# RWKV-7 recurrence of a hybrid decoder layer: each head on its own 64 rows, with block-diagonal operands

## The chip, the cores and the metric

The kernel runs on one core of a Trainium2 chip. The time is the device time in microseconds (us) of one execution. It is given as the median of several runs. A profile is one further execution, recorded by the hardware profiler; its times come from that execution alone. The engines in it are PE (the matrix engine; PEld is its weight loading), DVE (vector), ACT (scalar), POOL (GpSimd) and SP, which here only starts transfers.

## The reference, cut to what matters

One decoder layer for 1024 new tokens (and 8 single-token sequences that are handled apart): RMSNorm, one input projection, three parallel head groups (RWKV-7, HGRN2, RG-LRU), one output projection, then a squared-ReLU MLP with 4096 hidden columns, and a last norm. The change touches the RWKV-7 group: 6 heads of 64 channels, with a 64 by 64 state per head.

```python
k = k * (1.0 + (a - 1.0) * k_a)
def step(S, inp):
    rt, wt, kt, vt, kkt, at = inp
    sa = jnp.einsum('bhvk,bhk->bhv', S, -kkt)
    S = S * wt[:, :, None, :] + sa[..., None] * (kkt * at)[:, :, None, :] + vt[..., None] * kt[:, :, None, :]
    return S, jnp.einsum('bhvk,bhk->bhv', S, rt)
S_T, out = lax.scan(step, S0, (tm(r_h), tm(w_h), tm(k_h), tm(v_h), tm(kk), tm(a_h)))
gn = ((out - mean) * lax.rsqrt(var + GN_EPS)).reshape(B, T, c) * ln_w + ln_b
bonus = (jnp.sum(r_h * k_h * r_k, -1, keepdims=True) * v_h).reshape(B, T, c)
return (gn + bonus) * g, S_T
```

## The kernel before

The layer runs in two stretches. In the **first**, `weave` (L83) mixes seven streams of work with a filler, which is the dense work of the projections: input projections `in`, output projections `out`, and the first two MLP tiles. The order of PE's instructions is the order in which `weave` issues them. It keeps a modelled PE clock `now`, which `mm` (L71) and `tr` (L76) advance, and every `yield D` in a stream says by how much of that clock the stream should come back later; until then other streams or dense products are issued. The instructions of DVE, ACT and POOL are put in order by the compiler's scheduler, and each engine then runs its own list strictly in that order. In the **second** stretch, the MLP (`up`, `dn`) and the last norm run with nothing to weave.

The dense products are float32 split into a high and a low half (`xh`, `xl`, `wh`, `wl`), three products of one pass each. All small products of the recurrence are plain float32; one such product shows up as two matmul records in the trace, called halves below.

The recurrence is worked in 12 parts: 3 pairs of heads times 2 halves of the sequence times 2 quarters of 256 tokens. A part has 4 chunks of 64 tokens (`C` = 64, `NQ` = 4). The channels of the two heads of a pair lie on rows 0 to 63 and 64 to 127. Four streams share a part:

- `rw_operands` (L491) makes the operands. It needs the inverse root of the sums of squares of k: a product `pc_kk`, the value `ir_kk` on DVE (L245), its power on POOL (L129), a copy `t` on DVE (L248), and two transposes on PE into `pb_kk`, which DVE reads at L517. The decay and rate parts are the products `pw` and `pa`, with 64 rows each of `waup`. Then `kb` holds the two scaled key-like operands for one chunk; `kbt` is their transpose (4 transposes, copied by ACT at L560), and `uv` gets the transpose of v.
- `rw_inverse` (L574) computes the masked 64 by 64 tables: `sc` (L591) from `kb` and `ar` with 8 products, each 64 rows by 128 columns; then 6 levels that multiply a 64 by 64 inverse together (`W`, copied by ACT at L621; `Y`, merged by DVE at L636). Last it makes `mv`, 8 products with v.
- `rw_chain` (L652) goes through the chunks in order, as each needs the state `st` of the one before. Each step has three places on PE with a DVE operation behind each: `ch` from `st` and `ar`, then DVE's `rh` (L670); `ch` from `rh` and `ym`, then DVE's copy into `uv` (L676); then three groups together: `uv` with `kbt` (the new state, DVE's `st` at L697, with POOL's `ws` at L691), `st` with `ar`, and `uv` with `sc` (the outputs). The 128 rows carry alternate chunks here: `brow` and `krow` say which 64 rows a chunk sits on. The state is a 128 by 128 tile with zeros off the diagonal.
- `rw_finish` (L713) normalises the outputs, transposes them (`oT`), and writes them into `mix`.

A PE instruction uses the array in a tile size (rows by columns, in the profile "128\*128", "64\*64" and so on). The dense products and the transposes use 128\*128. The small ones before use 64\*64, 128\*64, 64\*128 or 32\*32.

Weights are staged by `load_w` (L255): a raw float32 tile by DMA, a copy and a difference into the high and low half. The raw tile has two buffers.

Of the kernel before, what the change touches and what calls it, by code (L numbers as in the profile page):

```python
# [51 lines left out]
def kernel(ctx: ExitStack, tc: tile.TileContext, i, o):  # L52
# [172 lines left out]
    waup = const.tile([P, 384], F32, name="waup")  # L225
# [29 lines left out]
    def load_w(src, name, kt=KT, wpool=wpool, dst=None, parts=1):  # L255


        raw = wpool.tile([P, kt, P], F32, tag=f"raw{kt}", name=f"raw_{name}", bufs=2)
        wh, wl = dst or (wpool.tile([P, kt, P], F32R, tag=f"{q}{kt}", name=f"{q}_{name}", bufs=2) for q in ("wh", "wl"))
        for g in range(parts):  # L260
            ks = slice(g * kt // parts, (g + 1) * kt // parts)
            nc.sync.dma_start(raw[:, ks], src[:, ks])
            act(wh[:, ks], raw[:, ks], AF.Copy)  # L263
            if name in SOON:
                V.tensor_tensor(wl[:, ks], raw[:, ks], wh[:, ks], op=ALU.subtract)  # L265
# [182 lines left out]
    lora, rkv = {}, {}  # L448
    sm = {nm: hgp.tile([P, 3, NB], F32, name=f"sm_{nm}") for nm in "rkv"}
# [23 lines left out]
    rw_st = [[rwp.tile([P, P], F32, name=f"st{j}_{q}") for q in range(2)] for j in range(3)]  # L473
    for st in rw_st:
        for q in range(2):
            G.memset(st[q], 0.0)
    brow = (slice(64, 128), slice(0, 64))
    krow = (slice(0, 64), slice(64, 128))
# [6 lines left out]
    def units():  # L485

        for h in range(2):
            for c in range(NQ):
                yield c, h, brow[c % 2], slice(((c // 2) * 2 + h) * C, ((c // 2) * 2 + h) * C + C)

    def rw_operands(q):  # L491
# [20 lines left out]
        mm(pw[:, 0:QT], waup[0:64, jc], xwa[0:64, qs])  # L512
# [8 lines left out]
        mm(pa[:, 0:QT], waup[64:128, jc], xwa[64:128, qs])  # L521
# [16 lines left out]
        for c in range(NQ // 2):
            tr(pt[:, c * P:(c + 1) * P], v[:, q0 + c * P:q0 + (c + 1) * P], ident)
        pt4 = pt[:, 0:NQ // 2 * P].rearrange("p (c x) -> p c x", x=P)  # L540
        S.copy(uv[0:64, 0:NQ:2, :], pt4[0:64])
        S.copy(uv[64:128, 1:NQ:2, :], pt4[64:128])
        ck4 = "p (c x t) -> p c x t"
        V.scalar_tensor_tensor(t5, t3, 1.0, t4, op0=ALU.add, op1=ALU.mult)
        V.scalar_tensor_tensor(kb[:, :, 1:3, :], t5.rearrange(ck4, x=2, t=C), 0.5, t1.rearrange(ck4, x=2, t=C),
                               op0=ALU.mult, op1=ALU.mult)
        V.tensor_scalar(t3, t3, hka[:, j:j + 1], omka[:, j:j + 1], op0=ALU.mult, op1=ALU.add)
        V.tensor_tensor(t3, t3, k_, op=ALU.mult)
        V.tensor_tensor(kb[:, :, 0:4:3, :], t3.rearrange(ck4, x=2, t=C), t1.rearrange(ck4, x=2, t=C), op=ALU.mult)
# [10 lines left out]
        S.copy(kbt, pt.rearrange("p (c x) -> p c x", x=P))  # L560
# [5 lines left out]
        mm(pb, bones, t5)  # L566
# [3 lines left out]
        live[q] = dict(ee=ee, ar=ar, kb=kb, kbt=kbt, uv=uv, bo=bo)  # L570
# [3 lines left out]
    def rw_inverse(q):  # L574
# [4 lines left out]
        ar, kb, uv = (live[q][x] for x in ("ar", "kb", "uv"))  # L579

        sc = rwp.tile([P, 2 * NQ, P], F32, tag="sc", name=f"sc_{n}", bufs=3)
        ym, xm = (w2(nm, n, 3).rearrange("p (u t) -> p u t", t=C) for nm in ("ym", "xm"))
        (S.copy if q < 2 else G.tensor_copy)(ym, bc(id64[:, None, :], [P, NQ, C]))
        for h in range(2):
            hp = slice(h * 64, h * 64 + 64)
            pt = ps("ra", f"sc{h}_{n}")
# [17 lines left out]
        for l in range(1, 6):  # L604
# [4 lines left out]
            pt = ps("ra", f"W{l}_{n}")[:, 0:QT]  # L609
            pt3 = pt.rearrange("p (u t) -> p u t", t=C)  # L610
            for c, h, b, cc in units():
                if last:
                    u, b0 = cc.start // C, b.start
                    mm(pt3[b0 + 32:b0 + 64, u, 0:32], sc[b0:b0 + 32, 2 * c + h, 32:64], xm[b0:b0 + 32, u, 0:32])
                else:
                    mm(pt[b, cc], sc[b, 2 * c + h, 0:64], xmf[b, cc])
# [25 lines left out]

        yield D14
# [4 lines left out]
        live[q].update(sc=sc, ym=ym, xm=xm)  # L648
# [3 lines left out]
    def rw_chain(q):  # L652
# [4 lines left out]
        ee, ar, kbt, uv, sc, ym, xm = (live[q][x] for x in ("ee", "ar", "kbt", "uv", "sc", "ym", "xm"))  # L657
        pt = ps("ch", f"ch_{n}")
        po = pt[:, QT:2 * QT]
        for c in range(NQ):  # L660
            st = rw_state[j]
            b = brow[c % 2]
            first = st is None
            mv = xm[b, (c // 2) * 2:(c // 2) * 2 + 2, :].rearrange("p h v -> p (h v)")
            if first:
                rh = mv
            else:
                mm(pt[b, 0:P], ar[:, c, 0, :], st)
                rht = rwp.tile([P, P], F32, tag="rh", name=f"rh{c}_{n}", bufs=1)
                V.tensor_tensor(rht[b, :], pt[b, 0:P], mv, op=ALU.add)  # L670
                rh = rht[b, :]
# [6 lines left out]
            for h in range(2):  # L678
# [5 lines left out]
            for h in range(2):  # L684
                hp = slice(h * 64, h * 64 + 64)
                mm(out[:, hp], sc[:, 2 * c + h, 64:128], uv[:, c, hp], start=first, stop=first or h == 1)
            wc = ee[:, c, C:C + 1]
            sn = rw_st[j][c % 2]
            if not first:
                ws = rwp.tile([P, P], F32, tag="ws", name=f"ws{c}_{n}", bufs=2)  # L690
                G.tensor_scalar(ws, st, wc, 0.0, op0=ALU.mult, op1=ALU.add)  # L691
            for h in range(2):
                hp = slice(h * 64, h * 64 + 64)
                if first:
                    V.tensor_scalar(sn[hp, hp], pt[hp, P:P + 64], wc[hp], None, op0=ALU.mult)
                else:
                    V.scalar_tensor_tensor(sn[hp, hp], pt[hp, P:P + 64], wc[hp], ws[hp, hp], op0=ALU.mult, op1=ALU.add)  # L697
# [15 lines left out]
    def rw_finish(q):  # L713
# [5 lines left out]
        ot, sums, bo = (live[q][x] for x in ("ot", "sums", "bo"))  # L719
        V.tensor_scalar(sums[:, 0], sums[:, 0], -1.0 / 64.0, None, op0=ALU.mult)  # L720
        sq = small.tile([P, 64], F32, tag="gsq", name=f"gsq_{n}", bufs=1)
        for g in range(NQ):
            act(sq, ot[:, g * 64:(g + 1) * 64], AF.Square, bias=sums[:, 0, g:g + 1],
# [828 lines left out]
```

## Time and profile before

| | before |
|---|---|
| median of 3 runs | 1618.23 us (1614.12 to 1618.76) |
| the profiled execution | 1615.32 us |
| its span, first to last instruction | 1613.5 us |
| mean granted PE clock | 0.967 |
| PE busy, whole span | 95% |
| DVE, ACT, POOL busy, whole span | 48%, 39%, 23% |
| PE busy, DVE busy, ACT busy from 250 to 410 us | 154.8, 107.7, 79.0 of 160 us |
| PE busy, DVE busy, ACT busy from 890 us to the end | 714.0, 202.6, 225.1 of 723 us |

A profile line of a group reads: source line, engine, operation, what is written "<-" what is read (names without buffer numbers), the tile size on PE, the shape, the count, then busy time and the mean duration in ns, then idle time ahead of it and what ended it. A line of the timeline reads: start in us, duration in us, engine, line, operation, names, count. Durations of PE records overlap, since matmuls are pipelined: what one costs is the distance from start to start.

### The profile page before, as it was taken

What the parts mean: (1) busy time and instruction counts of PE and PEld (TensorE: products, weight loads), DVE (VectorE), ACT (ScalarE), POOL (GpSimd) and SP (SyncE); (2) the same over time, 40 slices, a digit from 0 to 9 for tenths busy, and PEclk for the clock granted to TensorE, in tenths of its full rate; (3) what the DMA queues carried; (4) which work ended last, traced back from release to release, by engine and by line L of the source; (5) the groups of instructions that cost most, each with busy time, mean ns of one, the idle gap of its engine ahead of it and who ended that gap; (6) DMA issues with size and microseconds to landing.
All of it is one profiled execution on the core that took longest, in us unless ns stands there. A gap on an engine that the chain in (4) does not pass through costs nothing. (4 is left out here: it accounts for less than half of the span.)

```text
span 1613.5 us, 29358 instructions
## 1 busy us (share of the span) xinstructions
PE 1534.4 (95%) x12158; PEld 1310.5 (81%) x12158; DVE 775.8 (48%) x1765; ACT 637.1 (39%) x1361; POOL 376.9 (23%) x492
## 2 busy tenths in 40 slices
PE   8879899999899999899987999999999999999997
PEld 6657677688788788777787889989898989899887
DVE  7476656775656676675465222222232222222224
ACT  4444633653445355355344323233232423233232
POOL 4462312322323423423222010111101010111111
PEclk8979989999799999999999999999999999999999
DMA  6524424333243434434433353545445353544342
GB/s 216 134 53 95 90 67 92 80 80 86 60 91 75 100 80 101 99 81 113 113 119 103 82 109 80 108 85 104 83 101 92 79 110 81 104 85 89 58 90 106
DMA packets 54501, 152.18 MB, mean 94 GB/s; under 512 B 7104, under 2 KB 7392, under 8 KB 54368
## 3 DMA queue, kind: packets, MB, share of 16 engines
q0 software_dynamic: 24416, 70.67, 26.3%
q1 hardware_dynamic: 29808, 79.61, 15.3%
q8 instruction: 95, 1.56, 0.4%
q14 instruction: 38, 0.31, 0.1%
q10 hardware_dynamic: 144, 0.04, 0.0%
HBM read 144.12 MB, written 6.17 MB: 93 GB/s over the span
## 5 line engine op out<-in xcount | busy, mean ns | idle before, releaser
L74 PE MATMUL in<-xh,wl_in 128*128 128x512 f32 (+3 forms) x648 | 226.3, 349 | 6.5 <-DMA wl_in<-in_w_in 6.5
L74 PE MATMUL in<-xl,wh_in 128*128 128x512 f32 (+3 forms) x648 | 224.4, 346 | 3.4 <-DVE xl L357 3.4
L74 PE MATMUL in<-xh,wh_in 128*128 128x512 f32 (+3 forms) x648 | 225.4, 348 | 0.0
L74 PE MATMUL dn<-hh,wl_w 128*128 128x264 f32 (+2 forms) x696 | 223.3, 321 | 0.2 <-DMA wl_w<-in_w 0.2
L74 PE MATMUL dn<-hh,wh_w 128*128 128x264 f32 (+2 forms) x696 | 223.0, 320 | 0.0
L74 PE MATMUL dn<-hl,wh_w 128*128 128x264 f32 (+2 forms) x696 | 223.0, 320 | 0.0
L1440 DVE TENSOR_TENSOR mix<-mix,dn 128x512 f32<-128x512 f32 (+2 forms) x192 | 98.4, 512 | 241.6 <-PE dn L74 241.6
L268 POOL DMA_DIRECT2D wl_w<-in_w x88 | 76.3, 874 | 577.3 <-ACT hh L1370 323.6
L263 ACT ACTIVATE wh_w<-raw_w 128x512 fp32r<-128x512 f32 (+1 forms) x90 | 70.6, 784 | 272.5 <-PE dn L74 224.5
L1369 DVE SCALAR_TENSOR_TENSOR rl<-up,rl 128x512 f32<-128x512 f32 (+2 forms) x96 | 49.6, 516 | 222.3 <-ACT rl L1368 222.3
L74 PE MATMUL up<-nxh,wh_w 128*128 128x264 f32 (+1 forms) x512 | 145.7, 285 | 1.5 <-DVE rl L1369 1.3
L74 PEld LDWEIGHTS in<-xh,wl_in 128*128 128x128 f32 x648 | 128.2, 198 | 22.5 <-DMA wl_in<-in_w_in 8.0
L74 PE MATMUL up<-nxl,wh_w 128*128 128x264 f32 (+1 forms) x512 | 145.0, 283 | 0.5 <-POOL nxl L1268 0.5
L74 PE MATMUL up<-nxh,wl_w 128*128 128x264 f32 (+1 forms) x512 | 145.2, 284 | 0.0
L74 PEld LDWEIGHTS dn<-hh,wl_w 128*128 128x128 f32 x696 | 131.0, 188 | 13.8 <-DMA wl_w<-in_w 3.8
L74 PEld LDWEIGHTS in<-xl,wh_in 128*128 128x128 f32 x648 | 127.8, 197 | 17.5 <-DVE xl L357 4.3
L74 PEld LDWEIGHTS in<-xh,wh_in 128*128 128x128 f32 x648 | 128.6, 198 | 15.8 <-issue 4.7
L74 PEld LDWEIGHTS dn<-hl,wh_w 128*128 128x128 f32 x696 | 131.1, 188 | 10.0
L74 PEld LDWEIGHTS dn<-hh,wh_w 128*128 128x128 f32 x696 | 131.2, 188 | 9.2
L74 PE MATMUL up<-nh,wl_w 128*128 128x512 f32 x256 | 102.7, 401 | 5.9 <-DMA wl_w<-in_w 5.9
L1368 ACT ACTIVATE rl<-up 128x512 f32<-128x512 f32 (+2 forms) x96 | 43.3, 451 | 152.4 <-PE up L74 152.4
L74 PE MATMUL up<-nh,wh_w 128*128 128x512 f32 x256 | 102.6, 401 | 0.0
(438 smaller groups left out, 3215.8 us busy)
## 6 DMA issues: line engine op xcount, KB each, us to landing
raw_in<-in_w_in SPq DMA_DIRECT2D x53, 512.0 KB, 3.4
wl_in<-in_w_in POOLq DMA_DIRECT2D x49, 512.0 KB, 5.6
raw_w<-in_w SPq DMA_DIRECT2D x32, 512.0 KB, 3.3
raw_w<-in_w SPq DMA_DIRECT2D x64, 256.0 KB, 2.7
wl_w<-in_w POOLq DMA_DIRECT2D x30, 512.0 KB, 5.4
wl_w<-in_w POOLq DMA_DIRECT2D x58, 256.0 KB, 4.1
raw_out<-in_w_out SPq DMA_DIRECT2D x16, 512.0 KB, 3.4
wl_out<-in_w_out POOLq DMA_DIRECT2D x8, 512.0 KB, 5.6
```

The lines of the kernel that those rows point to most:

```text
L74: PE.matmul(out, lhsT, rhs, start=start, stop=stop)
L263: act(wh[:, ks], raw[:, ks], AF.Copy)
L268: G.dma_start(wl[:, ks], src[:, ks], accum_op=ALU.add)
L1368: act(rl[:, :n], pt[:, :n], AF.Relu)
L1369: V.scalar_tensor_tensor(rl[:, :n], pt[:, :n], 0.0, rl[:, :n], op0=ALU.max, op1=ALU.mult)
L1440: V.tensor_tensor(x2[m][:, c0:c0 + n], x2[m][:, c0:c0 + n], pt[:, :n], op=ALU.add)
```

## The change

Each head stays on its own 64 rows throughout, and operands are put on a diagonal of two 64 by 64 blocks, with zeros beside them, so that one product of the whole 128 by 128 array serves both heads:

- `kz` (the two key operands), `az` and `yz` (copies of `ar`'s first half and of `ym`) are block diagonals. They exist once each, and their zero blocks are written once at the start. `wup` and `aup` are the two halves of `waup` with zeros in the other rows.
- In a step of the chain each of the three places is one product of 128 rows and 128 columns against 64 moving columns. The output products (`st` with `ar`, `mv` and `vr` with `sr`) leave the step and stand together at the part's end, 24 products of 64\*64.
- The products with v move: the product `mv` leaves the end of `rw_inverse` and runs beside `W` at level 1, and a new product `kt` with `vr`, scaled by the chunk's decay `wc`, beside `W` at level 2. The state update then adds that `kv` on POOL, in a second operation.
- Transposes: of v 4 for 2, of the keys 8 (`bt`, `kt`) for 4, of the output 4 for 2. ACT has new copies: v doubled into `bt`, two each for `vr`, `kt`, `yz`, `az`.
- The buffers of `raw8` and `ee` are fewer (2 to 1, 3 to 1), and six weight tiles of the last MLP block take other buffers.

The core of the diff:

```diff
-    rw_st = [[rwp.tile([P, P], F32, name=f"st{j}_{q}") for q in range(2)] for j in range(3)]
-    brow = (slice(64, 128), slice(0, 64))
-    krow = (slice(0, 64), slice(64, 128))
+    rw_st = [[rwp.tile([P, C], F32, name=f"st{j}_{q}") for q in range(2)] for j in range(3)]
+    kz = rwp.tile([P, 2, NQ, 2, C], F32, name="kz")
+    az = rwp.tile([P, NQ, 2, C], F32, name="az")
+    yz = rwp.tile([P, NQ, 2, C], F32, name="yz")
...
-        mm(pw[:, 0:QT], waup[0:64, jc], xwa[0:64, qs])
+        mm(pw[:, 0:QT], wup[:, jc], xwa[:, qs])
...
+        S.copy(bt.rearrange("p c (h t) -> p c h t", t=C), twice(v_))
+        for c in range(NQ):
+            tr(pt[:, c * P:(c + 1) * P], bt[:, c], ident)
+        heads_of(vr, pt)
...
+        for c in range(NQ):
+            tr(pt[:, c * P:(c + 1) * P], kz[:, 0, c].rearrange("p h t -> p (h t)"), ident)
+        S.copy(bt, pt.rearrange("p (c x) -> p c x", x=P))
+        yield D4
+        pt = ps("o", f"kt_{n}")
+        for c in range(NQ):
+            tr(pt[:, c * P:(c + 1) * P], kz[:, 1, c].rearrange("p h t -> p (h t)"), ident)
+        heads_of(kt, pt)
...
-                mm(pt[:, c * P:(c + 1) * P],
-                   kb[hp, c // 2, 2 * (c % 2):2 * (c % 2) + 2, :].rearrange("p x t -> p (x t)"),
-                   ar[hp, c, :, :].rearrange("p x t -> p (x t)"))
+                mm(pt[:, c * P:(c + 1) * P], kz[:, g, c].rearrange("p h t -> p (h t)"), ar[:, c].rearrange("p x t -> p (x t)"))
...
+            if l <= 2:
+                for c, h, b, cc in units():
+                    mm(px[b, cc], kv[b, c] if l == 1 else kt[b, c], vr[b, c])
...
-        pt = ps("ra", f"mv_{n}")[:, 0:QT]
-        for c, h, b, cc in units():
-            mm(pt[b, cc], sc[krow[c % 2], 2 * c + h, 0:64], uv[krow[c % 2], c, h * 64:h * 64 + 64])
-        S.copy(xmf, pt)
...
+        for h, b in enumerate(brow):
+            S.copy(yz[b, :, h], ym[b])
+            S.copy(az[b, :, h], ar[b, :, 0])
...
-                mm(pt[b, 0:P], ar[:, c, 0, :], st)
+                mm(pa, az[:, c].rearrange("p h t -> p (h t)"), st)
...
-            for h in range(2):
-                hc = slice(h * 64, h * 64 + 64)
-                mm(pt[b, hc], ym[b, (c // 2) * 2 + h, :], rh[:, hc])
-            V.tensor_copy(uv[b, c, :], pt[b, 0:P])
+            mm(pu, yz[:, c].rearrange("p h t -> p (h t)"), rh)
+            V.tensor_copy(mv[:, c], pu)
             yield D17
-            for h in range(2):
-                hp = slice(h * 64, h * 64 + 64)
-                mm(pt[hp, P:P + 64], kbt[:, c, hp], uv[:, c, hp])
-            out = po[krow[c % 2], (c // 2) * P:(c // 2) * P + P]
-            if not first:
-                mm(out, ar[:, c, 1, :], st, stop=False)
-            for h in range(2):
-                hp = slice(h * 64, h * 64 + 64)
-                mm(out[:, hp], sc[:, 2 * c + h, 64:128], uv[:, c, hp], start=first, stop=first or h == 1)
+            mm(pst, bt[:, c], mv[:, c])
...
+                G.tensor_scalar(ws, st, wc[:, c:c + 1], 0.0, op0=ALU.mult, op1=ALU.add)
+                G.tensor_tensor(ws, ws, kv[:, c], op=ALU.add)
+            V.scalar_tensor_tensor(sn, pst, wc[:, c:c + 1], ws, op0=ALU.mult, op1=ALU.add)
...
             if c == NQ - 1:
+                for c_, h, b, cc in units():
+                    terms = ([(ar[b, c_, 1], sts[c_][b])] if sts[c_] is not None else []) + [(sr[b, g, c_], x[b, c_]) for g, x in enumerate((mv, vr))]
+                    for u, (w, x) in enumerate(terms):
+                        mm(po[b, cc], w, x, start=u == 0, stop=u == len(terms) - 1)
```

What this does to the order of the instructions, at three places. First PE's list, in the second step of the first part's chain; in its rows an `in` row is a dense product, and the shape behind the names is that of the operand in rows by columns. Before:

```order
L74 MATMUL ch_0_0_1299<-rh_0_0_0_1356,ym_0_0_751 64x64 x2
L74 MATMUL in_0_0_1384<-xl_224,wh_in_0_1258 128x512
L74 MATMUL in_0_0_1384<-xh_216,wl_in_0_1259 128x512
L74 MATMUL in_0_0_1384<-xh_217,wh_in_0_1258 128x512
L74 MATMUL in_0_0_1384<-xl_225,wh_in_0_1258 128x512
L74 MATMUL gram_0_0_1403<-rq_188,kq_0_0_1330 64x2x32 x8
L74 MATMUL Y_0_0_1_1413<-ym_0_1_990,wm_0_0_1_1358 64x64 x8
L74 MATMUL ch_0_0_1299<-uv_0_0_639,kbt_0_0_638 64x64 x2
L74 MATMUL ch_0_0_1299<-st_0_176,ar_0_0_636 64x128
L74 MATMUL ch_0_0_1299<-uv_0_0_639,sc_0_0_750 64x64 x2
```

Now, the same step:

```order
L74 MATMUL ch_0_0_1356<-rh_0_0_0_1464,yz 128x64
L74 MATMUL in_0_0_1428<-xh_227,wh_in_0_1285 128x512
L74 MATMUL in_0_0_1428<-xl_235,wh_in_0_1285 128x512
L74 MATMUL in_0_0_1428<-xh_227,wl_in_0_1286 128x512
L74 MATMUL in_0_0_1428<-xh_228,wh_in_0_1285 128x512
L74 MATMUL W_0_0_1_1488<-xm_0_1_1096,sa_0_1_1094 64x64 x8
L74 MATMUL gram_0_0_1498<-rq_197,kq_0_0_1433 64x2x32 x8
L74 MATMUL pc_kk_0_0_1508<-bones,t_1_0_0_1473 128x2 x2
L74 MATMUL ch_0_0_1356<-mv_0_0_806,bt_0_0_646 128x64
```

The two products with `ym` are one with `yz`, and of the five products at the end of the step one is left; the products of the outputs have moved to the end of the part.

Second, POOL's list early on, where the power `ir_kk` for the second part stands. The `mix` rows with `xrb` are the input's normalisation for the second half of the sequence (eight multiplications, then eight scalings). Before:

```order
L891 TENSOR_SCALAR hf_0_624<-hf_0_624,nfA,fA 128x512
L346 TENSOR_TENSOR mix_69<-mix_69,xrb 128x520
L346 TENSOR_TENSOR mix_70<-mix_70,xrb 128x520
L129 TENSOR_TENSOR ir_kk_0_1_789<-ir_kk_0_1_789,mhalf 128x4
L346 TENSOR_TENSOR mix_71<-mix_71,xrb 128x520
```

Now:

```order
L349 TENSOR_TENSOR mix_76<-mix_76,xrb 128x520
L350 TENSOR_SCALAR mix_69<-mix_69,vt 128x520
L350 TENSOR_SCALAR mix_70<-mix_70,vt 128x520
L946 TENSOR_TENSOR kq_0_0_1065<-kq_0_0_1065,hf_0_632 128x256
L350 TENSOR_SCALAR mix_71<-mix_71,vt 128x520
L350 TENSOR_SCALAR mix_72<-mix_72,vt 128x520
L129 TENSOR_TENSOR ir_kk_0_1_846<-ir_kk_0_1_846,mhalf 128x4
```

The power stood behind two of the eight multiplications; it stands behind all eight, four scalings and one `kq` now.

Third, DVE's list at the copy `t` that follows this power and that PE's transposes `pb_kk` read. Rows of `lgq`, `lxb`, `lxc` and `lcar` belong to the RG-LRU stream, rows of `kq` and `rq` to HGRN2. Before:

```order
L1142 SCALAR_TENSOR_TENSOR lxc_0_666<-lgq_0_504,lxc_0_666 128x512
L591 TENSOR_TENSOR sc_0_0_750<-sc_0_0_0_796,cmask 128x4x128
L598 COPY_PREDICATED ym_0_0_751<-cmask,sc_0_0_750 64x256 x2
L248 COPY t_0_0_1_738<-ir_kk_0_1_789 128x256
L602 STREAM_TRANSPOSE xm_0_0_752<-ym_0_0_751 128x256
```

Now:

```order
L941 TENSOR_TENSOR kq_0_0_1159<-b_0_1052 128x512
L1167 TENSOR_SCALAR lgq_0_513<-lgq_0_513 128x512
L949 TENSOR_TENSOR rq_197<-kq_0_0_1159,hq_0_705 64x256 x2
L1169 SCALAR_TENSOR_TENSOR lgq_0_513<-lgq_0_513,lxc_0_679 128x512
L1171 SCALAR_TENSOR_TENSOR lxc_0_679<-lxb_0_511,lgq_0_513 128x512
L1175 SCALAR_TENSOR_TENSOR mix_75<-lgl_0_512,lxc_0_679 128x512
L1179 COPY lcar<-lxc_0_679 128x1
L251 COPY t_0_0_1_796<-ir_kk_0_1_846 128x256
```

The copy (L248, now L251) has moved behind the next level of HGRN2 (`kq_0_0_1159`, whose buffer is the one that `xrb` held, so that it follows the last of POOL's multiplications) and behind the end of the first RG-LRU piece, which includes a square root on ACT.

More of the change, by code (lines that the diff above doesn't have):

```diff
@@ L223 @@
     V.tensor_scalar(nsp2, sp2, -2.0, None, op0=ALU.mult)
-    waup = const.tile([P, 384], F32, name="waup")
+    wup, aup = (const.tile([P, 384], F32, name=nm) for nm in ("wup", "aup"))
+    G.memset(wup[64:128], 0.0)
+    G.memset(aup[0:64], 0.0)
     gup = const.tile([P, 384], F32, name="gup")
@@ L255, in load_w @@
     def load_w(src, name, kt=KT, wpool=wpool, dst=None, parts=1):
-        raw = wpool.tile([P, kt, P], F32, tag=f"raw{kt}", name=f"raw_{name}", bufs=2)
+        raw = wpool.tile([P, kt, P], F32, tag=f"raw{kt}", name=f"raw_{name}", bufs=1 if kt == KT else 2)
         wh, wl = dst or (wpool.tile([P, kt, P], F32R, tag=f"{q}{kt}", name=f"{q}_{name}", bufs=2) for q in ("wh", "wl"))
@@ L504, in ck, with heads_of @@
             return ap.rearrange("p (c t) -> p c t", t=C)
+        def heads_of(out, pt):
+            for h, b in enumerate(brow):
+                S.copy(out[b], pt[b].rearrange("p (c h x) -> p c h x", h=2, x=C)[:, :, h])
         r_, k_, v_ = r[:, qs], k[:, qs], v[:, qs]
-        t1, t2, t3, t4, t5 = (w2(f"t{u}", n, 1) for u in range(1, 6))
+        t1, t2, t3, t4 = (w2(f"t{u}", n, 1) for u in range(1, 5))
         act(t2, k_, AF.Square, scale=vec("kk", j))
         pw = ps("o", f"pw_{n}")
-        mm(pw[:, 0:QT], waup[0:64, jc], xwa[0:64, qs])
+        mm(pw[:, 0:QT], wup[:, jc], xwa[:, qs])
         act(t1, pw[:, 0:QT], AF.Tanh, bias=hw0[:, j:j + 1], scale=0.5)
@@ L535, in rw_operands @@
         act(t1, t2, AF.Exp, scale=-1.0)
+        V.tensor_copy(wc, ee[:, :, C])
         pt = ps("o", f"vT_{n}")
[L538 to L546, printed above, removed]
+        S.copy(bt.rearrange("p c (h t) -> p c h t", t=C), twice(v_))
+        for c in range(NQ):
+            tr(pt[:, c * P:(c + 1) * P], bt[:, c], ident)
+        heads_of(vr, pt)
+        V.scalar_tensor_tensor(t2, t3, 1.0, t4, op0=ALU.add, op1=ALU.mult)
+        for h, b in enumerate(brow):
+            V.scalar_tensor_tensor(kz[b, 0, :, h], ck(t2[b]), 0.5, ck(t1[b]), op0=ALU.mult, op1=ALU.mult)
         V.tensor_scalar(t3, t3, hka[:, j:j + 1], omka[:, j:j + 1], op0=ALU.mult, op1=ALU.add)
         V.tensor_tensor(t3, t3, k_, op=ALU.mult)
-        V.tensor_tensor(kb[:, :, 0:4:3, :], t3.rearrange(ck4, x=2, t=C), t1.rearrange(ck4, x=2, t=C), op=ALU.mult)
+        for h, b in enumerate(brow):
+            V.tensor_tensor(kz[b, 1, :, h], ck(t3[b]), ck(t1[b]), op=ALU.mult)
         V.scalar_tensor_tensor(ar[:, :, 0, :], ck(t4), -1.0, ee[:, :, 0:C], op0=ALU.mult, op1=ALU.mult)
@@ L569, in rw_operands @@
             free["pm"] += 3
-        live[q] = dict(ee=ee, ar=ar, kb=kb, kbt=kbt, uv=uv, bo=bo)
+        live[q] = dict(wc=wc, ar=ar, bt=bt, kt=kt, vr=vr, bo=bo)
         ev(("A2", q), L_EV)
@@ L621, in rw_inverse @@
                 S.copy(wm, pt)
+            if l <= 2:
+                px3 = px.rearrange("p (c t) -> p c t", t=C)
+                if l == 1:
+                    S.copy(mv, px3)
+                else:
+                    V.tensor_tensor(kv, px3, bc(wc[:, :, None], [P, NQ, C]), op=ALU.mult)
             yield D12
@@ L656, in rw_chain @@
         yield ("B", q)
-        ee, ar, kbt, uv, sc, ym, xm = (live[q][x] for x in ("ee", "ar", "kbt", "uv", "sc", "ym", "xm"))
+        wc, ar, bt, vr, sr, ym, mv, kv = (live[q][x] for x in ("wc", "ar", "bt", "vr", "sr", "ym", "mv", "kv"))
+        for h, b in enumerate(brow):
+            S.copy(yz[b, :, h], ym[b])
+            S.copy(az[b, :, h], ar[b, :, 0])
         pt = ps("ch", f"ch_{n}")
+        pa, pu, pst = (pt[:, u * C:u * C + C] for u in range(3))
         po = pt[:, QT:2 * QT]
+        sts = []
@@ L660, in rw_chain @@
+        yield D14
         for c in range(NQ):
             st = rw_state[j]
[L662 to L667, printed above, removed]
-                mm(pt[b, 0:P], ar[:, c, 0, :], st)
-                rht = rwp.tile([P, P], F32, tag="rh", name=f"rh{c}_{n}", bufs=1)
-                V.tensor_tensor(rht[b, :], pt[b, 0:P], mv, op=ALU.add)
-                rh = rht[b, :]
+            sts.append(st)
+            rh = mv[:, c]
+            if st is not None:
+                mm(pa, az[:, c].rearrange("p h t -> p (h t)"), st)
+                rh = rwp.tile([P, C], F32, tag="rh", name=f"rh{c}_{n}", bufs=1)
+                V.tensor_tensor(rh, pa, mv[:, c], op=ALU.add)
@@ L692, in rw_chain @@
[L692 to L697, printed above, removed]
+            mm(pst, bt[:, c], mv[:, c])
+            sn = rw_st[j][qt] if c == NQ - 1 else rwp.tile([P, C], F32, tag="st", name=f"st{c}_{n}", bufs=4)
+            ws = kv[:, c]
@@ L708, in rw_chain @@
+                live[q].update(ot=ot, raw=raw, sums=sums)
                 ev(("C", q), 0.5)
@@ L718, in rw_finish @@
         om = mix[j][:, hf * HT + qt * QT:hf * HT + qt * QT + QT]
-        ot, sums, bo = (live[q][x] for x in ("ot", "sums", "bo"))
+        ot, raw, sums, bo = (live[q][x] for x in ("ot", "raw", "sums", "bo"))
         V.tensor_scalar(sums[:, 0], sums[:, 0], -1.0 / 64.0, None, op0=ALU.mult)
@@ L1006, in hg_half @@
             pc = ad[:, c % 2, (c // 2) * C:(c // 2 + 1) * C]
-            sn = pool.tile([P, C], F32, tag="hst", name=f"hst{c}_{n}", bufs=10)
+            sn = pool.tile([P, C], F32, tag="hst", name=f"hst{c}_{n}", bufs=9)
             if st is None:
@@ L1455 @@
         if m < 6:
-            w = wpool.tile([P, 2, FB, P], F32R, tag=("raw8", "wh8", "wl8")[m % 3], name=f"w2_{m}", bufs=2)
+            tag = ("wh8", "wl8", "raw8", "wl8", "wh8", "last")[m]
+            w = (mlp if m == 5 else wpool).tile([P, 2, FB, P], F32R, tag=tag, name=f"w2_{m}", bufs=2 if tag[0] == "w" else 1)
             ws.append(load_w(w_down(b, m), f"w2_{b}_{m}", kt=FB, wpool=mlp, dst=(w[:, 0], w[:, 1])))
@@ L1523, in outputs @@
     sh = r["shift"].transpose(2, 1, 0).reshape(1 + NB, D)
-    wkv = r["p_wkv"].reshape(3, 2, 64, 2, 64)
-    wkv = np.stack([wkv[:, h, :, h] for h in range(2)], axis=1).reshape(1, 1, 6, 64, 64)
+    wkv = r["p_wkv"].reshape(1, 1, 6, 64, 64)
     lru = r["lru"].reshape(256, 36)
```

104 lines of the change are left out of this document (51 added, 53 removed).

## The prediction

> **What bounds the kernel now.** I read the page first: shares of the span and the chain of waits (its lines with the largest shares).
>
> ```profile
> span 1613.5 us, 29358 instructions
> PE 1534.4 (95%) x12158; PEld 1310.5 (81%) x12158; DVE 775.8 (48%) x1765; ACT 637.1 (39%) x1361; POOL 376.9 (23%) x492
> PE dn L74 22%; PE up L74 21%; PE out L74 2%; DMA wl_w<-in_w 1%; PE fin L78 0%; DMA raw_w<-in_w 0%; DVE nxl L1268 0%; ACT nxh L1266 0%; POOL fss L129 0%; DVE tt L1265 0%; ACT wh_w L263 0%; ACT yt L1420 0%; POOLq L1539 0%; ACT rl L1368 0%; DVE wl_out L265 0%
> ```
> (The busy line is one line of the page.) PE is the bound. The chain that ended last is MLP products (`dn`, `up`), and the change leaves these alone. So what the change can win or lose lies in the woven first stretch, and reaches the end as an earlier or later start of the MLP. There PE is nearly always at work, its list is fixed, and so a microsecond of PE work removed is a microsecond won, unless PE then waits for another engine. Where it waits now is told by the waits of PE in the first 930 us (name, the engine and line waited for, us in total, times, longest):
>
> ```profile
> PE pb_kk L78 <- DVE t L248: 10.7, 3, 8.9
> PE oT L78 <- DVE ot L728: 9.3, 6, 2.3
> PE ch L74 <- DVE rh L670: 7.7, 7, 4.1
> PE in L74 <- DMA wl_in<-in_w_in: 6.5, 4, 4.1
> ```
> Few of the recurrence's hand-offs make PE wait: 7 of 45 for `rh`, 6 of 12 for `oT`, 3 of 12 for `pb_kk`. But one wait, 8.9 us, is as long as a third of all that.
>
> **PE: the price of a small product.** The timeline of PE about two places of one chain step, and one place with products of the full array:
>
> ```profile
> 309.19 0.39 PE L74 MATMUL in<-xh,wl_in 128*128 128x512 f32 x1
> 309.51 0.43 PE L74 MATMUL ch<-st,ar 128*64 128x128 f32 x2
> 309.87 0.50 PE L74 MATMUL in<-xh,wh_in 128*128 128x512 f32 x1
> 310.22 0.39 PE L74 MATMUL in<-xl,wh_in 128*128 128x512 f32 x1
> ...
> 311.37 0.39 PE L74 MATMUL in<-xh,wh_in 128*128 128x512 f32 x1
> 311.60 0.40 PE L74 MATMUL in<-xl,wh_in 128*128 128x512 f32 x1
> 311.93 0.44 PE L74 MATMUL ch<-rh,ym 64*64 64x64 f32 x4
> 312.30 0.50 PE L74 MATMUL in<-xh,wl_in 128*128 128x512 f32 x1
> 312.64 0.40 PE L74 MATMUL in<-xh,wh_in 128*128 128x512 f32 x1
> ```
> ```profile
> 75.85 0.60 PE L78 MATMUL kbt<-ident,kb 128*128 128x128 f32 x4
> 76.28 1.08 PE L74 MATMUL xc<-ones,xsq 128*128 128x1 f32 x10
> 77.29 0.50 PE L74 MATMUL in<-xl,wh_in 128*128 128x512 f32 x1
> ```
> From start to start a dense product takes 0.23 us (311.37 to 311.60). From 309.19 to 310.22 are 1.03 us with two of them, so the visit for `ch` from `st` cost 0.57; from 311.60 to 312.64, 1.04, so the one from `rh` cost 0.58. Full-array products follow each other at 0.11 whether they have 128 columns (0.43 for 4 transposes) or one (1.01 for 10 halves), so I take 0.11 for a half of 64 columns too; a plain product, two halves, is then 0.22. If the two halves at 309.51 also take 0.22, **changing the tile size there and back costs 0.35**, 0.17 a change. That leaves 0.23 for the four halves at 311.93, 0.058 each. Where neighbours use different quarters of the array it is less:
>
> ```profile
> 341.70 0.29 PE L74 MATMUL in<-xh,wh_in 128*128 128x272 f32 x1
> 341.83 0.28 PE L74 MATMUL in<-xl,wh_in 128*128 128x272 f32 x1
> 342.04 0.68 PE L74 MATMUL W<-xm,sc 64*64 64x64 f32 x16
> 342.65 0.40 PE L74 MATMUL in<-xh,wl_in 128*128 128x272 f32 x1
> 342.89 0.28 PE L74 MATMUL in<-xh,wh_in 128*128 128x272 f32 x1
> ```
> 341.83 to 342.89 is 1.06; without two dense products (0.13 each) and 0.35 for the changes, 16 halves took 0.45, 0.028 each.
>
> [...]
>
> **PE: the sum.** By products (before to after, each count times the prices above):
> - The chain, 48 steps (45 with a state): 90 products `st` with `ar` (20.0 us), 96 with `ym` (10.9), 96 with `kbt` (7.9), 96 with `sc` (10.9) become 45 + 48 + 48 full ones at 0.22 (31.4) and 282 of 64\*64 at the parts' ends (27.6): **+9.3**.
> - Products with v: 192 more beside `W` at 2 x 0.029 (+11.1), 96 `mv` less (−6.3): **+4.8**.
> - Transposes: v +24, keys +48, output +24, 96 at 0.11: **+10.6**. The tables `sc` have as many products as before.
>
> So products alone add 24.7 us. Against this, counting along PE's two lists up to the first `dn` how often the tile size changes: 617 before, 346 after. The 271 that go, at 0.17 (their mix of sizes, at the rates of such places, gives 0.172), take **−46.6**. (Three visits less in each of 48 steps would be 288 by itself; many visits stood beside other small tiles, and so cost less than 0.35 before.) PE's need falls by **21.9**. Bounds: a half of 64 columns between 0.058 and 0.11 makes the 141 chain products cost 15 us less or nothing; a change between 0.12 and 0.18 makes 271 of them 33 to 49. So −8 to −39, and I keep −21.9.
>
> **One wait grows: `pb_kk` of the second part.**
>
> ```profile
> 97.18 0.66 PE L78 MATMUL pb_kk<-ident,t 128*128 128x128 f32 x2 [8.88 <-DVE t L248]
> ...
> 85.14 2.91 POOL L346 TENSOR_TENSOR mix<-mix,xrb 128x520 f32<-128x520 f32 x2
> 88.02 1.39 POOL L129 TENSOR_TENSOR ir_kk<-ir_kk,mhalf 128x4 f32<-128x4 f32 x1
> 89.38 9.75 POOL L346 TENSOR_TENSOR mix<-mix,xrb 128x520 f32<-128x520 f32 x6
> 99.11 0.86 POOL L347 TENSOR_SCALAR mix<-mix,vt 128x520 f32<-128x520 f32 x1
> 99.95 1.10 POOL L929 TENSOR_TENSOR kq<-kq,hf 128x256 f32<-128x256 f32 x1
> ```
> ```profile
> 95.67 1.36 DVE L248 COPY t<-ir_kk 128x256 f32<-128x256 f32 x1
> ...
> 102.13 1.68 DVE L932 TENSOR_TENSOR rq<-kq,hq 64x256 f32<-64x256 f32 x2
> ...
> 108.50 0.68 DVE L1152 SCALAR_TENSOR_TENSOR lgq<-lgq,lxc 128x512 f32<-128x512 f32 x1
> ...
> 109.44 1.21 DVE L1154 TENSOR_TENSOR_SCAN lxc<-lxb,lgq 128x512 f32<-128x512 f32 x1
> 110.57 0.66 DVE L924 TENSOR_TENSOR kq<-b 128x512 f32<-128x512 f32 x1
> ...
> 111.89 0.69 DVE L1158 SCALAR_TENSOR_TENSOR mix<-lgl,lxc 128x512 f32<-128x512 f32 x1
> ```
> ```profile
> 102.93 1.28 ACT L1151 ACT_TABLE_LOAD   x1
> ...
> 104.68 0.64 ACT L1151 ACTIVATE lgq<-lgq 128x512 f32<-128x512 f32 x1 [0.47 <-DVE lgq L1150]
> ```
> PE stood from 88.3 to 97.2 for the copy `t`. Two lists delay that copy now. POOL: eight multiplications instead of two end at 85.1 + 2.9 + 9.8 = 97.8; four scalings at 0.86, one `kq` (1.1) and the power (1.4) end at about 103.7. DVE: the copy stands behind the second `kq`, whose buffer comes free at 97.8. From there: `kq` 0.7; ACT's two exponentials on it (about 0.8), then the table load and root, 1.28 + 0.64, to 101.2, with `rq` beside it (1.7); then 0.68 + 1.21 + 0.69 and a tiny copy, to about 104; the copy itself 0.4 to 1.4. PE goes on at about 105, 8 us later than before, and comes there with 1 us more work done by then (the sum of PE's rows up to that place is 66.1 us, 65.1 before). So **+7.5 us**, with bounds 0 (the rows fall as they did) and +13 (every DVE row from `kq` on at the slow price that DVE had beside POOL here, as 1.36 for that copy).
>
> **Shorter cover elsewhere.** Between giving a result away and needing the answer PE now has less to do: from `st` to `rh` 1.83 us of work for 2.0, from `yz` to `bt` 1.8 for 2.2, a step's end to the next 3.6 for 4.1, `pc_kk` to `pb_kk` about 2.4 for 3.0. All this is summed along the two lists at the prices above. The 15 smaller waits of the rows quoted first (2, 6 and 7) would grow by some 0.4 us each: **+6**, with bounds 0 and +20 (0.2 us for each of some 100 hand-offs of the chain).
>
> **DVE, ACT, POOL and the rest: nothing.** DVE's list loses about as much as it gains (wide `st`, `kb` and `sc` rows against halves by head). ACT gets 84 more small operations, none of them larger than the copy of `kbt`, and POOL 45 small additions to `ws`. The group of that copy, and the busy times of a stretch in the middle (PE, PEld, DVE, ACT, POOL):
>
> ```profile
> L560 ACT COPY kbt<-kbt 128x512 f32<-128x512 f32 x12 | 7.1, 596 | 10.6 <-PE kbt L78 10.5
> ```
> ```profile
> 250.00:410.00 160.00, 154.76 (x1723) 125.80 (x1721) 107.67 (x277) 78.95 (x214) 46.61 (x65) 0.97 0.38 83
> ```
> 84 at 0.6 us are 50 us at most, in a stretch of some 890 us in which ACT is idle for half (81 of 160) and POOL for two thirds, beside a PE that is busy for 155 of 160. If that cover goes, its price is the upper end of the last term. The single `raw8` buffer delays raw loads to a copy's end, but the copy waited for `wh` buffers anyway: nothing, at most 2.
>
> Sum, against the profiled execution's own 1615.3: 1615.3 − 21.9 + 7.5 + 6 = 1606.9. The median of the runs is 2.9 above that execution, and the prediction is for a median: **1609.8**, say 1610.
>
> **The rivals.**
> 1. *All of the saving arrives; the waits stay as they are.* For it: 38 of 45 `rh` hand-offs never waited, and the scheduler's rows about 88 us could fall otherwise in time than in my sum. Against it: the moved rows of POOL. 1618.2 − 21.9 = 1596.
> 2. *Slower: the root's path becomes the bound in each part.* `pc_kk`, `ir_kk` on DVE, POOL's power, the copy, `pb_kk` is a path of four engines, and its cover shrinks to 2.4 us, while the power alone takes 1.4 and the copy up to 1.4. POOL's list has second `ws` rows in it now, ACT's more copies. If the other 11 parts wait 2.5 us each, 27.5: 1610 − 6 + 27.5 = 1631. It decides from 1.3 us a part, (21.9 − 7.5) / 11. Against it: the row `pb_kk` above, 3 waits in 12, 1.8 us in the two that are not the early one.
> 3. *Nothing arrives*: other engines' latency sets the woven stretch's length, and PE's saving turns into waits: 1618. Against it: PE's busy share in that row of the middle.
> [...]
>
> **How the numbers follow.** About 0.3%, 5 us, is what a measurement of this kernel can tell from no change: faster is below 1613.4, slower above 1623.1. My forecast, 1604 to 1616, 0.42; rival 1, 0.2; rival 2, 0.2; rival 3, 0.15; rival 4, 0.03. Faster: 0.2 + four fifths of 0.42 + a little of rival 3, 0.56. Slower: most of 2 and 4, 0.21. Same: the rest, 0.23. The range reaches from rival 1's 1596 to rival 2's 1631, without some of either's tails: 1595 to 1630.
>
> **What would show it.** Right: in the changed profile, chain products stand as 128\*128 at 0.22 a visit, with no gap in the dense rows; the first `dn` starts about 8 us earlier; `pb_kk`'s longest wait is about 16 us. Wrong: that wait unchanged (rival 1), `pb_kk` waits in most parts (rival 2), or `ch` and `W` waits that add up to 20 us (rival 3); a visit of a full-array product at much over 0.22 would break the sum itself.

## The result, and the profile after

| | before | changed |
|---|---|---|
| median, with the first comparison | 1617.32 us (4 runs) | 1596.47 us (4 runs, 1589.38 to 1598.82) |
| ratio | | 0.9866, 95% interval 0.9831 to 0.9901 |
| a second comparison, on one chip | 1615.9 us (14 runs) | 1591.56 us (4 runs), 0.9845 (0.9824 to 0.9866) |
| the profiled execution, its span | 1615.32, 1613.5 us | 1598.82, 1597.0 us |
| granted PE clock in these runs | 0.964 to 0.970 (the 14 runs) | 0.971 to 0.977 (all 8) |

It is 21 to 24 us faster; 8 were forecast. The page of the changed kernel, and the waits of its PE in the first 930 us:

```profile
span 1597.0 us, 30289 instructions
PE 1495.7 (94%) x12536; PEld 1317.3 (82%) x12536; DVE 760.7 (48%) x1789; ACT 674.1 (42%) x1445; POOL 391.2 (24%) x541
```
```profile
PE pb_kk L78 <- DVE t L251: 20.6, 7, 13.0
PE in L74 <- DMA wl_in<-in_w_in: 9.5, 5, 5.4
PE ch L74 <- DVE st L707: 8.6, 12, 2.1
PE up L74 <- DMA wl_w<-in_w: 5.9, 1, 5.9
PE oT L78 <- DVE ot L743: 5.4, 5, 3.9
PE out L74 <- DMA wl_out<-in_w_out: 5.1, 2, 3.7
PE pw L74 <- ACT lgq L1156: 4.3, 1, 4.3
```
PE has more instructions and is busy for 39 us less; ACT has 37 us more. The early wait for `pb_kk` has grown from 8.9 to 13.0 us, others have gone, and a new one stands in all 12 parts (`ch` for `st`). So the waits did not shrink. To see what did, the stretch up to the first `dn` product is taken apart: pauses between PE's instructions of more than 0.15 us, summed; half of the time that PE worked at half clock (an estimate of what that clock cost, from the dense product of 512 columns, which in the kernel before took 0.43 us there and 0.23 at full clock); and the rest, which is PE's work at full clock.

| us | before | changed | difference |
|---|---|---|---|
| first `dn` starts at | 925.6 | 907.8 | −17.8 |
| pauses of PE | 66.5 | 87.7 | +21.2 |
| lost to half clock while working | 44.9 | 31.9 | −13.0 |
| work at full clock | 812.0 | 785.8 | −26.2 |

(The rest, 2.2 and 2.5 us, lies ahead of the first instruction. From the first `dn` to the end the two differ by 1.3 us.) The gain is work and clock; more pauses give a good half of it back. A second profiled execution of the changed kernel, the first run below, has 85.0, 28.9 and 785.2 us in the last three rows. A visit of the chain in the changed kernel, by the timeline of PE:

```profile
578.14 0.28 PE L74 MATMUL in<-xh,wl_in 128*128 128x256 f32 x1
578.25 0.28 PE L74 MATMUL in<-xh,wh_in 128*128 128x256 f32 x1
578.37 0.33 PE L74 MATMUL ch<-st,az 128*128 128x64 f32 x2
578.51 0.36 PE L74 MATMUL in<-xl,wh_in 128*128 128x256 f32 x1
578.72 0.28 PE L74 MATMUL in<-xh,wl_in 128*128 128x256 f32 x1
```
From 578.25 to 578.72 are 0.47 us with two dense products of 0.12: the visit took 0.23 us, where it took 0.57 before. The early wait, as PE, POOL and DVE show it:

```profile
107.97 0.66 PE L78 MATMUL pb_kk<-ident,t 128*128 128x128 f32 x2 [12.99 <-DVE t L251]
```
```profile
81.42 11.74 POOL L349 TENSOR_TENSOR mix<-mix,xrb 128x520 f32<-128x520 f32 x8 [2.26 <-ACT xrb L346]
93.14 1.91 POOL L350 TENSOR_SCALAR mix<-mix,vt 128x520 f32<-128x520 f32 x2
95.02 1.26 POOL L946 TENSOR_TENSOR kq<-kq,hf 128x256 f32<-128x256 f32 x1
96.27 1.71 POOL L350 TENSOR_SCALAR mix<-mix,vt 128x520 f32<-128x520 f32 x2
97.94 1.44 POOL L129 TENSOR_TENSOR ir_kk<-ir_kk,mhalf 128x4 f32<-128x4 f32 x1
```
```profile
100.86 0.68 DVE L941 TENSOR_TENSOR kq<-b 128x512 f32<-128x512 f32 x1
...
105.61 1.23 DVE L1171 TENSOR_TENSOR_SCAN lxc<-lxb,lgq 128x512 f32<-128x512 f32 x1
...
107.55 0.28 DVE L251 COPY t<-ir_kk 128x256 f32<-128x256 f32 x1
```
POOL's power came at 97.9, behind all eight multiplications, four scalings and a `kq`, and was ready at 99.4. DVE read it 8 us later, after the HGRN2 and RG-LRU rows ahead of the copy. It is DVE's place in line, not POOL's, that ended last. The `kq` row itself did not wait for its buffer, which came free at 93.2: DVE had been at work since 83.5 without a pause, and came to it at 100.9.

### The profile page after: what moved, and what is told of

Read it like the earlier page. It is cut to its first block, busy times and chain, and to the rows that moved or that the text cites. A ratio compares the mean times of both kernels' runs of the same rounds, so it can differ in the third digit from the quotient of the medians.

```text
span 1597.0 us, 30289 instructions
## 1 busy us (share of the span) xinstructions
PE 1495.7 (94%) x12536; PEld 1317.3 (82%) x12536; DVE 760.7 (48%) x1789; ACT 674.1 (42%) x1445; POOL 391.2 (24%) x541
## 4 chain that ended last, share of the span: by engine, by line
PE 71%; DVE 8%; DMA 6%; issue 6%; ACT 5%; POOL 2%; POOLq 0%; ACTq 0%; DVEq 0%
PE up L74 22%; PE dn L74 19%; PE in L74 14%; PE ch L74 2%; PE W L74 2%; PE out L74 2%; PE Y L74 2%; DMA wl_in<-in_w_in 1%; PE gram L74 1%; DMA wl_w<-in_w 1%; DMA raw_in<-in_w_in 1%; PE sc L74 1%; DMA wl_out<-in_w_out 1%; DVE rq L949 1%; DMA raw_out<-in_w_out 1%
## 5 line engine op out<-in xcount | busy, mean ns | idle before, releaser
L74 PE MATMUL in<-xh,wl_in 128*128 128x512 f32 (+3 forms) x648 | 220.3, 340 | 10.9 <-DMA wl_in<-in_w_in 9.5
L74 PE MATMUL in<-xh,wh_in 128*128 128x512 f32 (+3 forms) x648 | 220.8, 341 | 0.0
L74 PEld LDWEIGHTS in<-xh,wl_in 128*128 128x128 f32 x648 | 126.4, 195 | 21.9 <-DMA wl_in<-in_w_in 10.9
L74 PEld LDWEIGHTS in<-xh,wh_in 128*128 128x128 f32 x648 | 125.7, 194 | 10.2 <-issue 0.2
L74 PE MATMUL up<-nh,wl_w 128*128 128x512 f32 x256 | 102.6, 401 | 5.9 <-DMA wl_w<-in_w 5.9
```

Of the source, the lines that this page charges most:

```text
L74: PE.matmul(out, lhsT, rhs, start=start, stop=stop)
```

## The experiments

**The change once more, beside the next three on one chip.** 

> The changed kernel itself, so that the other runs of this group stand beside it on the same chip. All theories: 1596 us median, 0.987 of the kernel before.

It gave 1591.56 us, as in the table above. The next three are read against its 0.9845.

**The early wait.** In the changed kernel, only the delay ahead of one pair of transposes:

```diff
-        yield D1
+        yield D1 + 13 * (name == "kk0_0_1")
```


> Only the place of one pair of transposes is moved: those into pb_kk of the second part are issued 13 us of PE's modelled clock later, so that dense products stand where PE waited 13.0 us. Theory (that wait is a plain loss at the end): the wait goes, nearly as much comes off the time, 8 to 12 us less than the changed kernel, about 1586. Rival (the second part was late anyway, and what is saved here is waited for later): 0 to 3 us less, other waits of PE grow by about 10 us.

1579.74 us, 0.9772 (0.9751 to 0.9792): 11.8 us less than the changed kernel beside it. Its waits of PE, the rows over 7 us:

```profile
PE in L74 <- DMA wl_in<-in_w_in: 15.3, 6, 6.3
PE ch L74 <- DVE st L707: 9.9, 12, 2.0
PE pb_kk L78 <- DVE t L251: 7.6, 4, 2.5
```
The 13 us are gone, 6 us of them came back as waits for weights, and the first `dn` starts at 889.3 us where the repeated changed kernel had it at 901.5: 8.7 us less of pauses, 4.1 less lost to half clock. The wait is a plain loss, and it costs clock besides.

**The tile size alone.** The chain's full-array products as pairs on the diagonal blocks, everything else as changed:

```diff
-                mm(pa, az[:, c].rearrange("p h t -> p (h t)"), st)
+                for h, b in enumerate(brow):
+                    mm(pa[b], az[b, c, h], st[b])
...
-            mm(pu, yz[:, c].rearrange("p h t -> p (h t)"), rh)
+            for h, b in enumerate(brow):
+                mm(pu[b], yz[b, c, h], rh[b])
...
-            mm(pst, bt[:, c], mv[:, c])
+            for h, b in enumerate(brow):
+                mm(pst[b], bt[b, c, h * C:h * C + C], mv[b, c])
```


> The 141 full-array products of the chain become pairs of 64*64 products on the diagonal blocks of the same operands; nothing else differs. Counted along PE's list, the tile size changes 531 times instead of 346, and PE's need up to the first dn product grows by 29 us (31 for the changes, a little less for the products). Theory (the gain is PE time, mostly tile changes): 20 to 29 us slower than the changed kernel, 1616 to 1625, the time of the kernel before. Rival (the gain is from the rearranged stages, not from the size of the tiles): at most 8 us slower.

1610.68 us (10 runs), 0.9963 (0.9947 to 0.9979): 19 us slower than the changed kernel, just under the theory's 20 and far from the rival's 8. One visit in its timeline of PE:

```profile
560.03 0.28 PE L74 MATMUL in<-xh,wl_in 128*128 128x256 f32 x1
560.24 0.33 PE L74 MATMUL ch<-st,az 64*64 64x64 f32 x4
560.50 0.40 PE L74 MATMUL in<-xh,wh_in 128*128 128x264 f32 x1
560.74 0.29 PE L74 MATMUL in<-xl,wh_in 128*128 128x264 f32 x1
```
0.71 us less two dense products of 0.12 are 0.47, twice the full-array visit, though four halves on alternate blocks are the cheaper arithmetic (0.03 each, below). In its profiled execution, the slowest of the ten with 1623.88 us, PE's work at full clock was 803.5 us, 18 more than the changed kernel, not 29. The count of changes was right, 531 for 346; what the expectation had too small is what pairs save as products. By the prices of the blocks below that is 141 x (0.225 − 2 x 0.059) = 15 us, and 31 − 15 = 16. Read the other way, (17.7 + 15.1) / 185 puts a change of tile size at 0.18 us, an estimate beside the 0.17 of the prediction's sum.

**Twice the copies on ACT.**

```diff
-            S.copy(yz[b, :, h], ym[b])
-            S.copy(az[b, :, h], ar[b, :, 0])
+            for _ in range(2):
+                S.copy(yz[b, :, h], ym[b])
+                S.copy(az[b, :, h], ar[b, :, 0])
```


> The 48 new ACT copies into yz and az are made twice, some 17 us more of ACT. Theory (ACT's copies lie beside PE work): within 3 us of the changed kernel. Rival (ACT is on the chain's path): 8 to 17 us slower, and PE's waits for ch and W grow by that.

1597.38 us, 0.9886 (0.9868 to 0.9904): 5.8 us slower, between the two. ACT's new copies are not free: of the time of the added ones some three tenths comes through, and the prediction had nothing. They take 19 us here (48 at 0.40), about half of the 37 that the change adds to ACT. In the profiled execution PE's pauses sum to 89.0 us, 4.0 more than in the repeated changed kernel.

**The outputs back in the steps.** The loop over `units()` that forms the outputs stands in each step for that chunk alone, instead of at the part's end:

```diff
+            for c_, h, b, cc in units():
+                if c_ == c:
+                    terms = ([(ar[b, c_, 1], sts[c_][b])] if sts[c_] is not None else []) + [(sr[b, g, c_], x[b, c_]) for g, x in enumerate((mv, vr))]
+                    for u, (w, x) in enumerate(terms):
+                        mm(po[b, cc], w, x, start=u == 0, stop=u == len(terms) - 1)
```


> The changed kernel with the output products back in each step of the chain, six 64*64 products a step, as soon as that step's values are there; the part's end has none. The tile size changes 407 times on PE's list instead of 346, 10 us more of PE at 0.17 each; the products are the same. Theory (tile changes set the price): 8 to 15 us slower than the changed kernel. Rival (that they leave the chain's steps gains nothing by itself): within 4 us.

1612.22 us (12 runs), 0.9967 (0.9949 to 0.9985): 1.0 to 1.2% above the changed kernel's two ratios, 16 to 20 us, more than expected. In its profiled execution PE's work was 807.1 us, 21.9 more than the repeated changed kernel; 14.9 of that stand on the instructions that change the tile size (407 of them for 346, 102.6 us for 87.8). So the regrouping of the outputs is worth about as much as the full-array products are; neither half alone gives more than 0.4%. Together they exceed the whole gain, for the change also adds work: transposes, products with v, ACT's copies, and the longer waits.

**The early wait in the kernel before.** The same one-line edit there.

> The kernel before, with the one pair of transposes into pb_kk of the second part issued 13 us of PE's modelled clock later, as in the run with the changed kernel. Theory (the early wait is a plain loss in both kernels, 8.9 us here and 13.0 there): 6 to 10 us less than the kernel before, about 1608, and the change alone, without this wait, is worth 26 to 30 us. Rival: no change, since the older chain is later anyway.

1610.57 us, 0.995 (0.9928 to 0.9971): 7 us less, as expected. Its profile agrees only in part: the wait for `pb_kk` is gone, but `W` waits 11.6 us for DVE's `xm` (longest 7.7) in its place, and all pauses sum to 64.5 us, 2 less than before; the rest of the gain in that execution is clock and work. Taking both kernels with the edit, 0.9772 to 0.995, the change is worth 1.8%, some 29 us.

**What lowers the clock.** In the kernel before, PE worked at half clock also where it had not paused. Two neighbouring windows of its profile (PE busy, PEld, DVE, ACT, POOL, then the granted clock):

```profile
430.70:434.10 3.40, 3.40 (x55) 2.98 (x54) 0.46 (x2) 0.47 (x1) 0.00 (x0) 1.00 0.80 198
434.10:437.50 3.40, 3.40 (x16) 3.16 (x16) 2.97 (x9) 0.49 (x2) 1.43 (x2) 0.50 0.00 0
```
PE was busy throughout the first, with small tiles and one-column products (55 records), and the next had half the clock. So, to see which products lower the clock where PE does not pause, four blocks of products were put into the MLP, one in each of four kernels, their results unused (from 1000 to 1013 us, ahead of the blocks, PE was busy for 13.00 of 13.00 us in each):

```diff
+            if (b, m) == (1, 3):
+                pt = ps("ch", "probe")
+                for u in range(240):
+                    w = brow[u % 2]
+                    mm(pt[w, 0:64], ident[w, w.start:w.start + 64], x2[m][w, 0:64])
```


> The changed kernel with 240 additional 64*64 products (diagonal blocks, alternately) in one block within the MLP, some 14 us without a pause, their results unused. [...]

> The same place, with 80 additional full-array products of 64 columns instead, some 13 to 18 us. [...]

The third has 64 times `mm(pt[:, 0:1], ident, x2[m][:, 0:1])`, the fourth 48 products, alternately of 64\*64 and of the full array.

> The probe within the MLP again: 64 full-array products of one column each, some 14 us without a pause, their results unused. Small tiles alone left the clock at full speed. [...]

> The same place, with 24 products of 64*64 and 24 of the full array in turn, all of 64 columns, so that every product changes the tile size. By 0.35 us for there and back the block takes 13 to 15 us, and measures the price of a change by itself: 0.17 us each. [...]

Each of the four was executed once. For each, the block's row in the timeline, and behind it a window that lies within the block (busy times, then the granted clock):

```profile
1026.15 14.21 PE L74 MATMUL probe<-mix,ident 64*64 64x64 f32 x480
```
```profile
1028.00:1034.00 6.00, 6.00 (x212) 6.00 (x210) 0.00 (x0) 0.00 (x0) 0.65 (x1) 1.00 0.49 86
```
```profile
1017.29 17.97 PE L74 MATMUL probe<-mix,ident 128*128 128x64 f32 x160
```
```profile
1028.00:1034.00 6.00, 6.00 (x57) 6.00 (x55) 0.00 (x0) 0.00 (x0) 0.00 (x0) 1.00 0.00 0
```
```profile
1013.91 24.50 PE L74 MATMUL probe<-mix,ident 128*128 128x1 f32 x128
```
```profile
1028.00:1034.00 6.00, 6.00 (x29) 6.00 (x30) 0.00 (x0) 0.00 (x0) 0.00 (x0) 0.50 0.00 0
```
```profile
1015.41 21.02 PE L74 MATMUL probe<-mix,ident 64*64 64x64 f32 x96
```
```profile
1028.00:1034.00 6.00, 6.00 (x26) 4.59 (x25) 0.00 (x0) 0.00 (x0) 0.00 (x0) 0.50 0.00 0
```
(The 96 records of the fourth show under the first one's tile size.) PE is busy for all 6 us in each. Small tiles alone leave the clock at 1.00; so do full-array products of 64 columns. One-column products bring 0.50, and so do products that change the tile size each time. In the last two the half clock lasted from 3 to 6 us after the block's start until 5 to 6 us after its end (the mean clock was 1.00 in both from 1013 to 1017 us, 0.50 and 0.69 from 1017 to 1027, 0.78 and 0.93 from 1040 to 1050). Pauses are not needed: from 1013 to 1027 us, where the clock fell, PE was busy for 14.00 of 14.00 us in both.

Prices by the way. A plain float32 half beside a dense product, in the kernel before:

```profile
428.65 0.59 PE L74 MATMUL bonus<-t,bones 128*128 128x256 f32 x2
428.89 0.47 PE L74 MATMUL in<-xl,wh_in 128*128 128x256 f32 x1
429.20 0.28 PE L74 MATMUL in<-xh,wl_in 128*128 128x256 f32 x1
429.32 0.28 PE L74 MATMUL in<-xh,wh_in 128*128 128x256 f32 x1
```
From 428.65 to 429.20 are 0.55 us with two float32 halves and one dense product of 0.12, all of 256 columns; so a half took 0.215, 0.84 ns a column for the dense product's 0.46.

From the blocks: 0.059 us for a 64\*64 product on alternate blocks (14.21 / 240), 0.225 for a full-array one of 64 columns (17.97 / 80). The fourth block was meant to give the price of a change too, but its clock fell, and it doesn't: 21 us hold by estimate 13.2 to 21 us of full-speed time, depending on whether a change slows as well.

**Two steps further.** On top of the later `pb_kk` transposes, the output block issued before the last `bt` product, and then one more microsecond between `pc_kk` and `pb_kk` in the other 11 parts:

```diff
+            if c == NQ - 1:
+                for c_, h, b, cc in units():
...
             mm(pst, bt[:, c], mv[:, c])
...
-        yield D1 + 13 * (name == "kk0_0_1")
+        yield D1 + (13 if name == "kk0_0_1" else 1)
```


> The kernel with the later pb_kk transposes, and in it the block of output products at each part's end issued before the last bt product instead of behind it. In the profile that block waits 12 times for DVE's st, 9.9 us in all, since it stands behind a product whose result DVE is reading from the same bank. Theory: these waits go and 5 to 9 us come off, to about 1572. Rival: the block waits for mv there instead, as long: no change.

> The run with the outputs first, and in it one more microsecond of PE work between pc_kk and pb_kk in the other 11 parts. In the profile with the later transposes 4 of these waits are left, 7.6 us in all. Theory (that path is short of cover in some parts): 2 to 5 us less than without. Rival (PE's other work is as short there): no change, or slower by up to 3 where the later operands arrive later.

The first gave 0.9789 (0.9761 to 0.9817), no better than 0.9772 without it. The 12 waits of `ch` for `st` are gone from its profile, and the wait behind them has grown from 2.4 us to this:

```profile
PE oT L78 <- DVE ot L744: 15.7, 4, 7.9
```
With the second, 0.9771 (0.9744 to 0.9797), 1578.02 us: 5.7 us less than the first by the medians, a little over the theory's 2 to 5, and 2.9 by the ratios; but the intervals overlap, and it is no better than the kernel with the one-line edit alone. So the best of these kernels is at 0.977, 12 us below the changed one by the first of these comparisons, and all of that is the early wait.

## Why the prediction was right and wrong

The direction was right, and the range held the time at its edge, though the second comparison's 1591.56 lies below it; the forecast gain was less than half of the measured one. By its steps, in the two profiled executions:

- **PE's work: −21.9 forecast, −26.2 measured.** The mechanism, fewer changes of tile size against dearer products, is the one that the run with pairs shows. The visit of 0.22 us came as 0.23. Taking the pairs' run by the blocks' prices gives 0.18 us for a change, which speaks against the fourth rival, changes of tile size at 0.12 us or less. What was mis-sized is the block at the parts' ends, 27.6 us in the sum, about 0.10 a product: the three kinds of product there took 21.0 us together at full clock, 0.074 each. That neighbours in it use different quarters of the array, as with the 16 halves of `W` (0.028 each), is the author's guess at the reason; no run tests it.
- **The clock: no term, −13.0 measured.** This is the step that failed. The sum took every price at full clock and left the 45 us that half clock cost before as they were. By work and pauses alone, the terms that it had, the stretch would have gained 26.2 − 21.2 = 5.0 us, for 8.4 forecast; most of the 17.8 is the term that it did not have, so that the direction came out so clearly is partly luck. The runs of the two kernels lie apart by clock, as the first table shows; the other two groups' 30 runs of the kernel before reach from 0.962 to 0.972, so the edges touch. With either half of the change taken back, part of the clock goes too: the medians are 0.974 for the repeated changed kernel, 0.9715 with the pairs, 0.971 with the outputs in the steps, and 0.967 and 0.966 for the kernel before beside them. That changes of tile size can lower it without a pause is shown by the fourth probe (0.50, with PE busy for 6.00 of 6.00 us); that they did so here, in the places where the kernel before lost clock without a pause, is argued from the table and such windows, not isolated by a run.
- **The early wait: +7.5 forecast; the wait grew by 4.1 us, and one of 4.3 appeared just ahead of it (`pw` for ACT), +8.4 together.** The order of the two lists was read rightly, and the RG-LRU rows of DVE were the last to arrive, as in the sum. But PE went on at 108, for 105 in the sum: it had DVE start on `kq` when the buffer came free, at 97.8, and DVE came there at 100.9 by its own earlier rows, 3 us later.
- **Shorter cover elsewhere: +6 forecast; all other pauses grew by 12.8** (21.2 − 8.4). Most of the difference is a wait that no step had: at each part's end the outputs stand right behind a product whose result DVE reads from the same tile `ch`, from other columns of it (8.6 us, 12 times). The wait is gone where the outputs come first; that the shared tile causes it is read from the kernel, and no run gives the outputs a tile of their own. The moved block was counted on PE, but not what it is queued behind.
- **ACT's copies at nothing:** not shown to be right: one half of them, made twice, cost 5.8 us. What the first ones cost is not measured.
- The first rival's 1596 us is where the time came out, but not for its reason: it had the waits stay as they were. They grew by 21 us, and the clock and a larger saving made up for it: that the time fell there is a coincidence. The third rival, PE's saving turned into waits, holds for 21.2 of the 26.2 us, spread over more waits than `ch` and `W`. The second rival, the root's path in each part, has 7.6 us in 6 waits beside the early one, not 27.5. Small tiles for the chain's products lose here by 19 us, in the run that differs in nothing else.

## What to carry to other kernels

Where small products are strewn among large ones, price the visit, not the product: here two changes of tile size cost more than a half-empty array (0.35 us by estimate for the two, where a full-array product of 64 columns took 0.225 and two of 64\*64 0.12), and gathering what must stay small in one block was worth as much (16 to 20 us, for 19). Before summing a saving, ask what the edit does to the clock (13.0 us here), and look for half clock at places where the engine never paused. And read the place of each step in every in-order list that it depends on: one copy that had fallen behind other streams' rows cost half as much as the whole change brought (11.8 us, of 24.3 in that comparison), and one line took it back.

## What the runs showed of the hardware

The granted clock fell to one half with PE busy without a pause, when what it did were one-column products or changes of tile size at every product (0.50 in both blocks); with 64\*64 products on alternate blocks, or full-array ones of 64 columns, it stayed at full (1.00 in both). Ahead of the first `dn` in the kernel before, the half clock came in 17 stretches, of 3.4, 6.8, 10.2, 13.7 and 17.1 us. The profile's busy time doesn't tell when it comes: both blocks that lowered the clock show 6.00 of 6.00 us, as do the two that did not. By what measure of PE's work the clock is granted, no run shows.
